# A final norm's weight multiplied in at PSUM, and two block products made to run together

## The chip, the core and the metric

One core of a Trainium2 chip runs the whole kernel in one launch. The engines are TensorE (PE; its weight loads are PEld), VectorE (DVE), ScalarE (ACT), GpSimd (POOL) and SyncE (SP, which here only issues DMAs). The metric is the device time of one execution in microseconds, as the median of three runs.

## The reference

One layer of a backbone is applied to 128 context tokens and 512 latent tokens (640 in all, width 2048), with fp32 weights, and a last RMSNorm follows:

```python
def _layer(x, mod, s0, shift_fn, lp):
    sh1, sc1, g1, sh2, sc2, g2 = jnp.split(mod, 6, axis=-1)
    h = _rmsnorm(x, lp['norm1_g']) * (1.0 + sc1) + sh1
    p = h @ lp['w_in']
    o_a, s_fin = _rwkv7_bidir(shift_fn(p[..., :C_SHIFT], lp['mu_shift']), s0, lp)
    o_b = _chunk_gmlp(jax.nn.gelu(p[..., C_SHIFT:]), lp)
    x = x + g1 * (jnp.concatenate([o_a, o_b], axis=-1) @ lp['w_out'])
    h = _rmsnorm(x, lp['norm2_g']) * (1.0 + sc2) + sh2
    ff = (jax.nn.silu(h @ lp['w_ffn_gate']) * (h @ lp['w_ffn_up'])) @ lp['w_ffn_down']
    return x + g2 * ff, s_fin
...
    y_prompt = _rmsnorm(x_ctx, final_norm_g)
    y_sample = _rmsnorm(x_lat, final_norm_g)
```

`_rmsnorm(x, g)` is `x * rsqrt(mean(x*x) + 1e-6) * g`: a scale for each token, and a weight for each of the 2048 columns. `_rwkv7_bidir` holds a scan over tokens in both directions in which each step changes a 64 by 64 state for each of 16 heads; `_chunk_gmlp` mixes tokens in chunks of 128.

## The kernel before

Large products are made with split operands: a fp32 weight tile is cast to a shorter format on ACT (`hi`), DVE subtracts to get the rest (`lo = raw - hi`), and three products hi·hi, hi·lo, lo·hi are summed in PSUM. TensorE thus waits for a pair of `hi` (ACT) and `lo` (DVE) for each weight tile.

**The first stage (to about 1160 us of the span)** runs the input projection: `win` makes "wide" products of 320 tokens (`big`), in blocks of weight columns. Between them, generators ("mixers") issue the small work of the scan. `between(k)` is called after each group of three wide products, and gives each mixer a budget. A generator yields the estimated cost of what it issued. A yield of -1.0 ends its turn, and the next one comes only at a call with `many` set, which is every twelfth wide product. A framework with a scheduler of its own then puts the instructions of each engine in an order, so neighbours in the code need not be neighbours on the engine.

The scan is worked out in chunks of 64 tokens. For each chunk a 64 by 64 triangular matrix is inverted: `solve` inverts blocks of 16 on DVE, and `merge` joins them to 32 and then to 64. `merge` runs for 8 pairs of heads and both directions, 16 times. For each, `blk(lhs, rhs)` makes 32 by 32 products for ten chunks into a PSUM tile of the pool `pt_`, which has two buffers and also serves the transposes of other generators and the spatial products. The steps are: `M1` from `blk(A1, Tn)`, copied by ACT; `blk(TT, M1)` added into `Tn` by DVE (L832); `blk(M1, TT)` added into `TF` by DVE (L837, L838); then the two products to 64 (`pM2`, L845, and `pT2`, L854), with ACT copies.

**The feed-forward part** uses one level of Strassen's method: `seven` makes seven products instead of eight, in the order `PORD = (1, 2, 3, 7, 5, 6, 4)`, and a hook for each product takes it out of PSUM, three or four products later (`lag`). POOL subtracts weight tiles for the combined ones (L1516). The down projection runs in six chunks of its inner dimension. The accumulators of the 8 output steps `n` (256 columns each) lie in `acc`, seven slots of 320 columns for each `n`.

**In the last chunk** (n from 7 to 0, about 3160 to 3285 us) `filled` first brings the accumulated slots back into PSUM (ACT, L1900), and the hook is `Last`. It puts the four quadrants together in two tiles `cd` (L1852, L1857, L1860 to L1863, L1868), adds the residual `x1d`, which SP loads for each step (`out`, L1841), and in hook 6 loads 256 columns of the last norm's weight, repeated over the partitions, into a free slot of `acc` (L1866). One step later `rows` transposes the two tiles to token rows in PSUM (`prd`, L1881), copies them to `acc` on ACT (L1882), and squares them on ACT with a sum for each token (L1885).

**The end** adds the sums of squares (L1946), takes the inverse root on POOL (L134), and scales. Each of ten half rows (128 tokens by 1024 columns) is multiplied by its token's scale and by the weight: six by one DVE instruction (L1958), four by ACT (L1955) and then POOL (L1956). SP stores each (L1959).

Of the kernel before, what the change touches and what calls it, by code (L numbers as in the profile page):

```python
# [86 lines left out]
def flow_step(ctx: ExitStack, tc, x_prompt, x_sample, state_rwkv, c, c_ctx, w_mod, b_mod,  # L87
# [706 lines left out]
    def merge(p, d2):  # L794

        GB = pairs[p].GB
        for gq in range(8):
            b = 16 * (gq % 2)
            BQ.dma_start(TB[16 * gq:16 * gq + 16, :, :, :, b:b + 16].rearrange("p d c w b -> p (d c w) b"),
                         d2[gq].rearrange("d c w a b -> a (d c w) b"))  # L800
        for h in range(2):
            base = 64 * (1 - h)
            for d in range(2):
                S.copy(A1_[base:base + 16, d, :, 16:32], GB[d][base:base + 16, :, 16:32])
                S.copy(A1_[base + 32:base + 48, d, :, 16:32], GB[d][base + 32:base + 48, :, 48:64])
        yield HOLD
        for d in range(2):
            GBd = GB[d]
            TF = bp.tile([P, NCH, CH], F32, tag="TF", name="TF")
            for h in range(2):  # L810
                G.memset(TF[hi32(h), :, 0:32], 0.0)
            Tn, TT, A1 = TB[:, d, :, 0, :], TB[:, d, :, 1, :], A1_[:, d]

            def blk(lhs, rhs, rows=range(4)):
                ps = pt_.tile([P, NCH, 32], F32, tag="pt", name="pblk")
                for cc in range(NCH):
                    for a_ in rows:
                        s = slice(32 * a_, 32 * a_ + 32)
                        TE.matmul(ps[s, cc, :], lhs[s, cc, :], rhs[s, cc, :], start=True, stop=True,  # L819
                                  tile_position=(32 * a_, 32 * a_))  # L820
                return ps

            M1 = bp.tile([P, NCH, 32], F32, tag="M1", name="M1")
            yield -1.0
            ps = blk(A1, Tn)
            S.copy(M1, ps)
            yield 1.6
            yield -1.0

            ps = blk(TT, M1, (0, 2))  # L830
            for h in range(2):
                V.tensor_add(Tn[lo32(h)], ps[lo32(h)], Tn[lo32(h)])  # L832
            yield 1.6
            yield -1.0
            ps = blk(M1, TT)
            for h in range(2):
                V.tensor_add(TF[lo32(h), :, 0:32], ps[lo32(h)], TT[lo32(h)])  # L837
                V.tensor_add(TF[hi32(h), :, 32:64], ps[hi32(h)], TT[hi32(h)])  # L838
            yield 1.7
            M2 = bp.tile([P, NCH, 32], F32, tag="M1", name="M2")  # L840
            yield -1.0
            ps = pt_.tile([P, NCH, 32], F32, tag="pt", name="pM2")
            for cc in range(NCH):
                for h in range(2):
                    TE.matmul(ps[hi32(h), cc, :], GBd[lo32(h), cc, 32:64], Tn[lo32(h), cc, :],  # L845
                              start=True, stop=True, tile_position=(64 * (1 - h), 64 * (1 - h) + 32))
            for h in range(2):
                S.copy(M2[hi32(h), :, :], ps[hi32(h), :, :])
            yield 1.2
            yield -1.0  # L850
            ps = pt_.tile([P, NCH, 32], F32, tag="pt", name="pT2")
            for cc in range(NCH):
                for h in range(2):
                    TE.matmul(ps[lo32(h), cc, :], M2[hi32(h), cc, :], TF[hi32(h), cc, 32:64],  # L854
                              start=True, stop=True, tile_position=(64 * (1 - h) + 32, 64 * (1 - h)))
            for h in range(2):
                S.copy(TF[lo32(h), :, 32:64], ps[lo32(h), :, :])
            yield 1.2
            BQ.dma_start(d_S[p, :, d, :, F_T:F_T + CH], TF)
            merged.append(p)  # L860
        G.memset(TB[:, :, :, 0, 0:16], 0.0)
# [936 lines left out]
    acc = dn.tile([P, 8, 7 * HALF], F32, name="acc")  # L1798
    sse = dn.tile([P, NT, 8], F32, name="sse")
    slot = lambda n, i: acc[:, n, (i - 1) * HALF:i * HALF]  # L1800

    def seg(h):

# [28 lines left out]
    class Last:  # L1832
# [11 lines left out]
        def __call__(self, o, p):  # L1844
            n, ps = self.n, self.ps
            ps[PORD[o]] = p
            if o == 1:
                self.xs = xqs.pop(n)
                self.cs = [xap.tile([P, T], F32, tag=next(ctags), name="cd") for _ in range(2)]
                self.tp = tp = xap.tile([P, 2, HALF], F32, tag="rs2", name="tp")  # L1850
                S.copy(tp[:, 0], ps[1])
                V.tensor_add(self.cs[0][:, t1], ps[2], tp[:, 0])  # L1852
                self.out(0, 0)
            elif o == 4:
                act = self.cs[1]
                S.copy(act[:, t2], ps[5])
                V.tensor_add(act[:, t1], ps[3], act[:, t2])  # L1857
            elif o == 5:
                act, pa, pq = self.cs[1], self.tp[:, 0], self.tp[:, 1]
                V.tensor_add(pq, ps[6], pa)  # L1860
                V.tensor_add(act[:, t1], act[:, t1], pq)
                V.tensor_add(pq, ps[7], pq)
                V.tensor_add(act[:, t2], act[:, t2], pq)  # L1863
                self.out(1, 0)
            elif o == 6:
                nc.sync.dma_start(acc[:, n, 5 * HALF:5 * HALF + 256],  # L1866
                                  final_norm_g[n * 256:(n + 1) * 256].partition_broadcast(P))
                V.tensor_add(self.cs[0][:, t2], ps[4], self.tp[:, 1])  # L1868
                later.append((2, lambda: (self.out(1, 1), self.out(0, 1))))
                later.append((ROWO, self.rows))  # L1870
                load_x1(n - 1)

        def rows(self):

            n, cs = self.n, self.cs
            for q0 in (0, 2, 4):
                nt = min(2, NT - q0)
                pr = pP.tile([P, 2, 256], F32, tag="P", name="prd")
                for t in range(nt):
                    for m in range(2):  # L1880
                        TE.transpose(pr[:, t, m * P:(m + 1) * P], cs[m][:, (q0 + t) * P:(q0 + t + 1) * P], ident)  # L1881
                S.copy(acc[:, n, q0 * 256:(q0 + nt) * 256].rearrange("p (t c) -> p t c", c=256), pr[:, 0:nt])  # L1882
                for t in range(nt):
                    junk = dn.tile([P, 256], F32, tag="junk", name="junk2")
                    S.activation(junk, pr[:, t], AF.Square, accum_out=sse[:, q0 + t, n:n + 1])  # L1885
# [60 lines left out]
    V.tensor_reduce(out=rs, in_=sse, axis=AX.X, op=ALU.add)  # L1946
    V.tensor_scalar(rs, rs, 1.0 / D, RMS_EPS, op0=ALU.mult, op1=ALU.add)
    rsqrt(rs, rs)
    fg = acc[:, :, 5 * HALF:5 * HALF + 256]
    for t in range(NT):  # L1950
        for h in range(2):
            out = fin.tile([P, 4, 256], F32, tag=f"out{h}", name="out")
            src, f = (ap[:, 4 * h:4 * h + 4] for ap in (acc[:, :, t * 256:(t + 1) * 256], fg))
            if t == 1 or t == 3:
                S.activation(out, src, AF.Copy, scale=rs[:, t:t + 1])  # L1955
                G.tensor_tensor(out=out, in0=out, in1=f, op=ALU.mult)  # L1956
            else:
                V.scalar_tensor_tensor(out=out, in0=src, scalar=rs[:, t:t + 1], in1=f, op0=ALU.mult, op1=ALU.mult)  # L1958
            nc.sync.dma_start(yrows(t)[:, h * 1024:h * 1024 + 1024], out.rearrange("p n c -> p (n c)"))  # L1959
    xax.close()  # L1960

# [28 lines left out]
```

## Time and profile before

| what | us |
|---|---|
| median of 3 runs | 3313.23 (3312.97 to 3317.33) |
| the profiled execution | 3309.26, its span 3307.5 |
| TensorE busy | 3147.1 |
| DVE busy | 2441.1 |
| ACT busy | 1457.4 |
| POOL busy | 1264.7 |
| mean granted TensorE clock | 0.981 of full speed |

Rows of the profile read as follows. In a timeline: start, duration, engine, source line, operation, output<-inputs, shape, count, and in brackets the idle time before it with what ended it. In a listing by line or tile: shortest/median/longest duration in ns, then the first and last start. In a table of waits: the sum, the number and the longest. Names leave out buffer numbers (`P` is a PSUM bank of the feed-forward part, `pM` is `pM2`, `t` is `t3`). In the rows of an order (not a time) `[waits ...]` names the engines or queues whose semaphores an instruction waits for.

### The profile page before, as it was taken

What the parts mean: (1) busy time and instruction counts of PE and PEld (TensorE: products, weight loads), DVE (VectorE), ACT (ScalarE), POOL (GpSimd) and SP (SyncE); (2) the same over time, 40 slices, a digit from 0 to 9 for tenths busy, and PEclk for the clock granted to TensorE, in tenths of its full rate; (3) what the DMA queues carried; (4) which work ended last, traced back from release to release, by engine and by line L of the source; (5) the groups of instructions that cost most, each with busy time, mean ns of one, the idle gap of its engine ahead of it and who ended that gap; (6) DMA issues with size and microseconds to landing.
All of it is one profiled execution on the core that took longest, in us unless ns stands there. A gap on an engine that the chain in (4) does not pass through costs nothing.

```text
span 3307.5 us, 72626 instructions
## 1 busy us (share of the span) xinstructions
PE 3147.1 (95%) x28216; PEld 2907.3 (88%) x28216; DVE 2441.1 (74%) x4356; ACT 1457.4 (44%) x3190; POOL 1264.7 (38%) x1114
## 2 busy tenths in 40 slices
PE   6899999999999999999899999999999999999996
PEld 3688787788877888888899999999999999999996
DVE  4548667876876678768887887777877788877787
ACT  3334444444443444334644444444444444444365
POOL 0001122212222113333156566566566555555543
PEclk8899999999999999999999999999999999999998
DMA  8767676677677588735543443433433454553453
GB/s 319 240 183 217 172 209 187 163 206 200 184 190 210 142 272 277 239 119 159 160 123 102 131 124 105 131 120 109 128 119 114 126 183 147 159 163 119 133 159 118
DMA packets 739376, 550.90 MB, mean 167 GB/s; under 512 B 140968, under 2 KB 673464, under 8 KB 730200
## 3 DMA queue, kind: packets, MB, share of 16 engines
q1 hardware_dynamic: 726712, 532.57, 53.8%
q0 software_dynamic: 9984, 13.13, 1.8%
q8 instruction: 222, 3.64, 0.5%
q14 instruction: 122, 1.00, 0.1%
q10 hardware_dynamic: 2336, 0.57, 0.1%
HBM read 437.79 MB, written 110.95 MB: 166 GB/s over the span
## 4 chain that ended last, share of the span: by engine, by line
PE 74%; DVE 11%; issue 6%; DMA 4%; POOL 3%; ACT 2%; DVEq 0%; SPq 0%; ACTq 0%; POOLq 0%
PE P L1605 15%; PE P L1604 15%; PE P L1603 15%; PE big L187 5%; PE big L189 4%; PE big L188 4%; PE pG L635 2%; PE pm L880 2%; DMA wt<-in_w_mod_dram 1%; DVE lo L1393 1%; PE big L1012 1%; PE pblk L819 1%; PE pXT L652 1%; DVE mx L780 1%; DMA raw<-in_w_out_dram 1%
## 5 line engine op out<-in xcount | busy, mean ns | idle before, releaser
L1603 PE MATMUL P<-xo,hi 128*128 128x320 f32 x2352 | 727.6, 309 | 3.3 <-ACT hi L1392 3.3
L1605 PE MATMUL P<-xo,lo 128*128 128x320 f32 x2352 | 727.6, 309 | 2.0 <-DVE lo L1393 1.9
L1604 PE MATMUL P<-xo,hi 128*128 128x320 f32 x2352 | 727.4, 309 | 0.0
L1393 DVE TENSOR_TENSOR lo<-raw,hi 128x512 fp32r<-128x512 f32 x532 | 511.7, 965 | 171.3 <-ACT hi L1392 165.9
L1392 ACT CAST hi<-raw 128x512 fp32r<-128x512 f32 x532 | 330.8, 622 | 495.9 <-PE P L1604 395.9
L187 PE MATMUL big<-h_hi,hi 128*128 128x320 f32 x1376 | 451.7, 328 | 6.6 <-ACT h_hi L343 3.7
L1603 PEld LDWEIGHTS P<-xo,hi 128*128 128x128 f32 x2352 | 442.1, 188 | 3.5 <-ACT hi L1392 3.5
L1605 PEld LDWEIGHTS P<-xo,lo 128*128 128x128 f32 x2352 | 441.9, 188 | 2.8 <-DVE lo L1393 2.8
L1604 PEld LDWEIGHTS P<-xo,hi 128*128 128x128 f32 x2352 | 442.1, 188 | 0.0
L189 PE MATMUL big<-h_hi,lo 128*128 128x320 f32 x1376 | 435.7, 317 | 2.6 <-DVE lo L166 2.5
L188 PE MATMUL big<-h_lo,hi 128*128 128x320 f32 x1376 | 435.4, 316 | 0.5 <-DVE h_lo L344 0.5
L1516 POOL TENSOR_TENSOR raw<-raw 128x512 f32<-128x512 f32 x252 | 407.5, 1626 | 14.3 <-DVE lo L1393 2.7
L1605 PE MATMUL P<-xd,lo 128*128 128x320 f32 x1232 | 384.0, 312 | 14.9 <-DVE lo L1393 14.6
L1603 PE MATMUL P<-xd,hi 128*128 128x320 f32 x1232 | 382.6, 311 | 4.4 <-ACT P L1900 1.9
L1604 PE MATMUL P<-xd,hi 128*128 128x320 f32 x1232 | 381.2, 309 | 0.0
L166 DVE TENSOR_TENSOR lo<-raw,hi 128x512 fp32r<-128x512 f32 x268 | 185.3, 694 | 214.1 <-ACT hi L165 202.8
L187 PEld LDWEIGHTS big<-h_hi,hi 128*128 128x128 f32 x1376 | 263.7, 192 | 72.9 <-issue 47.7
L1392 ACT CAST hi<-rawd 128x512 fp32r<-128x512 f32 (+1 forms) x288 | 169.0, 588 | 243.5 <-PE P L1604 204.9
L165 ACT CAST hi<-raw 128x512 fp32r<-128x512 f32 x268 | 165.5, 619 | 245.5 <-PE big L188 116.3
L189 PEld LDWEIGHTS big<-h_hi,lo 128*128 128x128 f32 x1376 | 263.5, 192 | 8.1 <-DVE lo L166 4.3
L188 PEld LDWEIGHTS big<-h_lo,hi 128*128 128x128 f32 x1376 | 264.2, 192 | 6.9 <-issue 3.5
L1605 PEld LDWEIGHTS P<-xd,lo 128*128 128x128 f32 x1232 | 231.8, 188 | 21.2 <-DVE lo L1393 21.1
(378 smaller groups left out, 6300.9 us busy)
## 6 DMA issues: line engine op xcount, KB each, us to landing
wt<-in_w_mod_dram SPq DMA_DIRECT2D x96, 1024.0 KB
raw<-in_w_ffn_gate_dram SPq DMA_DIRECT2D x182, 256.0 KB
raw<-in_w_ffn_up_dram SPq DMA_DIRECT2D x182, 256.0 KB
rec<-d_S SPq DMA_DIRECT2D x80, 576.0 KB
raw<-in_w_in_dram SPq DMA_DIRECT2D x172, 256.0 KB
rawd<-in_w_ffn_down_dram SPq DMA_DIRECT2D x128, 256.0 KB
raw<-in_w_out_dram SPq DMA_DIRECT2D x96, 256.0 KB
xd<-d_os SPq DMA_DIRECT2D x66, 320.0 KB
```

The source lines that it names most:

```text
L165: S.copy(hi, raw)
L166: V.tensor_sub(lo, raw, hi.bitcast(F32))
L187: TE.matmul(halves[hf], hi[:, k, :], h_hi[:, kb, s], start=(kb == 0), stop=False)
L188: TE.matmul(halves[hf], hi[:, k, :], h_lo[:, kb, s], start=False, stop=False)
L189: TE.matmul(halves[hf], lo[:, k, :], h_hi[:, kb, s], start=False, stop=(kb == KB - 1))
L635: TE.matmul(two[h][:, cc - c0, :], XZ[:, cc, h, :, :].rearrange("p s t -> p (s t)"), R[:, cc, :, :].rearrange("p s t -> p (s t)"), start=T ...
L1392: S.copy(hi[:, 0:nk], raw[:, 0:nk])
L1393: V.tensor_sub(lo[:, 0:nk], raw[:, 0:nk], hi[:, 0:nk].bitcast(F32))
L1516: G.tensor_tensor(out=o[:, 0:nk], in0=p[:, 0:nk], in1=q[:, 0:nk], op=ALU.subtract)
L1603: TE.matmul(ps, hi[:, k, :], xk[:, 0, :], start=f, stop=False)
L1604: TE.matmul(ps, hi[:, k, :], xk[:, 1, :], start=False, stop=False)
L1605: TE.matmul(ps, lo[:, k, :], xk[:, 0, :], start=False, stop=l)
```

## The change

- In `merge`, `blk(TT, M1)` and `blk(M1, TT)` are issued together, and DVE's additions of both follow. The yields between them go.
- In `Last`, the weight's load moves from hook 6 to hook 4.
- In `rows`, ACT's copy out of PSUM becomes a DVE multiply by the weight, with the same output.
- At the end each half row is only scaled by token: the second halves by ACT, the first by DVE. POOL takes no part.

```diff
-            ps = blk(TT, M1, (0, 2))
+            ps, ps2 = blk(TT, M1, (0, 2)), blk(M1, TT)
             for h in range(2):
                 V.tensor_add(Tn[lo32(h)], ps[lo32(h)], Tn[lo32(h)])
-            yield 1.6
-            yield -1.0
-            ps = blk(M1, TT)
+            ps = ps2
             for h in range(2):
                 V.tensor_add(TF[lo32(h), :, 0:32], ps[lo32(h)], TT[lo32(h)])
                 V.tensor_add(TF[hi32(h), :, 32:64], ps[hi32(h)], TT[hi32(h)])
-            yield 1.7
+            yield 3.3
...
+    fg = lambda n: acc[:, n, 5 * HALF:5 * HALF + 256]
...
             elif o == 4:
+                nc.sync.dma_start(fg(n), final_norm_g[n * 256:(n + 1) * 256].partition_broadcast(P))
                 act = self.cs[1]
...
             elif o == 6:
-                nc.sync.dma_start(acc[:, n, 5 * HALF:5 * HALF + 256],
-                                  final_norm_g[n * 256:(n + 1) * 256].partition_broadcast(P))
                 V.tensor_add(self.cs[0][:, t2], ps[4], self.tp[:, 1])
...
-                S.copy(acc[:, n, q0 * 256:(q0 + nt) * 256].rearrange("p (t c) -> p t c", c=256), pr[:, 0:nt])
+                V.tensor_tensor(out=acc[:, n, q0 * 256:(q0 + nt) * 256].rearrange("p (t c) -> p t c", c=256),
+                                in0=pr[:, 0:nt], in1=fg(n).unsqueeze(1).to_broadcast([P, nt, 256]), op=ALU.mult)
                 for t in range(nt):
                     junk = dn.tile([P, 256], F32, tag="junk", name="junk2")
                     S.activation(junk, pr[:, t], AF.Square, accum_out=sse[:, q0 + t, n:n + 1])
...
-    fg = acc[:, :, 5 * HALF:5 * HALF + 256]
     for t in range(NT):
         for h in range(2):
             out = fin.tile([P, 4, 256], F32, tag=f"out{h}", name="out")
-            src, f = (ap[:, 4 * h:4 * h + 4] for ap in (acc[:, :, t * 256:(t + 1) * 256], fg))
-            if t == 1 or t == 3:
+            src = acc[:, 4 * h:4 * h + 4, t * 256:(t + 1) * 256]
+            if h:
                 S.activation(out, src, AF.Copy, scale=rs[:, t:t + 1])
-                G.tensor_tensor(out=out, in0=out, in1=f, op=ALU.mult)
             else:
-                V.scalar_tensor_tensor(out=out, in0=src, scalar=rs[:, t:t + 1], in1=f, op0=ALU.mult, op1=ALU.mult)
+                V.tensor_scalar_mul(out, src, rs[:, t:t + 1])
```

The lines move by up to three: L1841 is L1840 in the changed kernel, L1393 is L1391, L1885 is L1884, and L1880 is the new multiply.

## The prediction

> **What bounds the kernel now.** I read the page first: TensorE is busy for 95% of the span and holds 74% of the chain that ended last, VectorE (DVE) 11%. So a change matters where TensorE waits for something, and after its last product.
>
> ```profile
> PE 3147.1 (95%) x28216; PEld 2907.3 (88%) x28216; DVE 2441.1 (74%) x4356; ACT 1457.4 (44%) x3190; POOL 1264.7 (38%) x1114
> ...
> PE 74%; DVE 11%; issue 6%; DMA 4%; POOL 3%; ACT 2%; DVEq 0%; SPq 0%; ACTq 0%; POOLq 0%
> ```
>
> The change touches three places, so I then took busy times by stretch: the stage with the merges (300 to 1160 us), a full output step of the last chunk (16.08 us) and its last one, and the end.
>
> ```profile
> 300.00:1160.00 860.00, 817.49 (x9808) 697.52 (x9807) 615.32 (x1227) 380.60 (x831) 184.22 (x285) 0.98 0.69 187
> 3231.96:3248.04 16.08, 15.23 (x103) 14.44 (x102) 13.77 (x23) 10.39 (x32) 5.31 (x4) 1.00 0.27 81
> 3264.10:3280.00 15.90, 15.57 (x107) 15.02 (x106) 12.38 (x24) 11.17 (x35) 2.66 (x2) 1.00 0.17 51
> ...
> 3289.00:3290.00 1.00, 0.00 (x0) 0.00 (x0) 1.00 (x1) 1.00 (x2) 1.00 (x1) 0.50 0.46 184
> 3296.00:3297.00 1.00, 0.00 (x0) 0.00 (x0) 1.00 (x1) 0.00 (x0) 1.00 (x1) 0.50 1.01 401
> 3305.00:3306.00 1.00, 0.00 (x0) 0.00 (x0) 0.00 (x0) 0.00 (x0) 0.00 (x0) 0.50 0.95 377
> ```
>
> After the clock of the first column come PE, PEld, DVE, ACT, POOL, granted clock, DMA share, GB/s. TensorE is idle for 42.5 us of the merge stage, 5%. In the last chunk DVE is nearly as full as TensorE. In the end only DVE, POOL and the stores work, and the stores are at 401 GB/s when they run.
>
> **The end.** The timeline of the end, by engine:
>
> ```profile
> 3281.78 1.26 DVE L1841 SCALAR_TENSOR_TENSOR cd<-cd,modc,x1d 128x64 f32<-128x64 f32 x4
> 3282.06 0.39 ACT L1885 ACTIVATE junk<-prd 128x256 f32<-128x256 f32 x1
> 3282.57 0.39 ACT L1885 ACTIVATE junk<-prd 128x256 f32<-128x256 f32 x1
> 3283.57 0.58 ACT L1882 COPY acc<-prd 128x512 f32<-128x512 f32 x1 [0.52 <-PE prd L1881]
> 3285.71 0.20 DVE L1946 TENSOR_REDUCE rse<-sse 128x5 f32<-128x40 f32 x1 [2.67 <-ACT junk L1885]
> 3287.40 15.69 DVE L1958 SCALAR_TENSOR_TENSOR out<-acc,rse 128x1024 f32<-128x1024 f32 x6 [1.29 <-POOL rse L134]
> 3288.62 12.19 POOL L1956 TENSOR_TENSOR out<-out,acc 128x1024 f32<-128x1024 f32 x4 [1.26 <-ACT out L1955]
> 3288.75 14.70 SPq L1959 DMA_DIRECT2D out_dram<-out  x10
> ...
> L1958 DVE SCALAR_TENSOR_TENSOR out<-acc,rse x6: 1272/3356/3455, 3287.4 to 3301.8; 128x1024 f32<-128x1024 f32 x6
> ...
> L1955 ACT ACTIVATE out<-acc,rse x4: 1132/1132/1149, 3287.4 to 3290.5; 128x1024 f32<-128x1024 f32 x4
> ...
> L241 DVE TENSOR_SCALAR xall<-xall,rs x5: 1286/1286/1289, 11.0 to 26.9; 128x2048 f32<-128x2048 f32 x5
> ```
>
> One DVE product of this size took 1.27 us alone and 3.36 us beside POOL, so ten outputs were spread over 15.7 us and the ten stores followed them. The change takes the second operand and POOL away. L241 is the new DVE form at twice the width, 1.29 us, so one is 0.65 us; five on DVE take 3.3 us, five on ACT 5 x 1.13 = 5.7 us, side by side. Then the stores bound: 10 x 0.524 MB at 401 to 406 GB/s are 12.9 to 13.1 us. From the first scale to the end that is 0.65 + 0.07 to the issue + 0.8 until bytes flow (issued at 3288.75, and only 0.46 of the DMA engines' time in the stretch from 3289) + 12.9 + 1.6 after the last byte = 16.0 us, where it was 3307.5 - 3287.4 = 20.1: 4.1 us less.
>
> Ahead of it something is lost. The order of ACT for the last output step shows it; L1884 is the square that was L1885:
>
> ```order
> L1899 COPY P_40345<-acc 128x320 [waits DVE_49,PE_49]
> L1884 ACTIVATE junk_40325,sse<-prd 128x256 [waits DVE_49]
> L1884 ACTIVATE junk_40327,sse<-prd 128x256 [waits Activation_49]
> L1884 ACTIVATE junk_40335,sse<-prd 128x256 [waits DVE_49,Activation_49]
> L1884 ACTIVATE junk_40337,sse<-prd 128x256 [waits Activation_49]
> L1884 ACTIVATE junk_40343,sse<-prd 128x256 [waits DVE_49,Activation_49]
> L1884 ACTIVATE junk_40396,sse<-prd 128x256 [waits DVE_49,Activation_49]
> ```
>
> In before, ACT copied the rows and squared them, waiting for nobody between; now the first square of each PSUM tile waits for DVE's multiply out of the same tile, and what is queued behind it on ACT (the next chunk's `hi` casts, the bank fills) waits too. In the last step DVE reaches that multiply when its four L1841 end, at 3283.04. The first multiply takes 0.60 us (below) and five squares at 0.51 (3282.06 to 3282.57) follow it: 3283.7 + 2.6 = 3286.3, where the reduction began at 3285.71: 0.6 us later. The end gives 4.1 - 0.6 = **-3.5**. Bounds: -4.6 if the squares were not held and only lost the copy ahead of them (0.5 us of the 0.58 of L1882); -2.6 with the stores 0.3 us and the squares 0.6 us slower.
> [...]
>
> **The last chunk.** One step of DVE, POOL and SP before:
>
> ```profile
> 3233.43 1.23 DVE L1841 SCALAR_TENSOR_TENSOR cd<-cd,modc,x1d 128x256 f32<-128x256 f32 x1
> 3234.57 1.58 DVE L1863 TENSOR_TENSOR cd<-cd,tp 128x320 f32<-128x320 f32 x1
> 3237.28 0.68 DVE L1393 TENSOR_TENSOR lo<-rawd,hi 128x512 fp32r<-128x512 f32 x1
> 3237.88 1.74 DVE L1841 SCALAR_TENSOR_TENSOR cd<-cd,modc,x1d 128x64 f32<-128x64 f32 x2
> 3239.54 1.78 DVE L1393 TENSOR_TENSOR lo<-t,hi 128x512 fp32r<-128x512 f32 x1
> 3241.24 0.67 DVE L1841 SCALAR_TENSOR_TENSOR cd<-cd,modc,x1d 128x64 f32<-128x64 f32 x2
> 3241.83 0.48 DVE L1852 TENSOR_TENSOR cd<-P,tp 128x320 f32<-128x320 f32 x1
> 3244.99 0.68 DVE L1841 SCALAR_TENSOR_TENSOR cd<-cd,modc,x1d 128x256 f32<-128x256 f32 x2 [1.48 <-DMA x1d<-d_x]
> 3248.04 0.49 DVE L1860 TENSOR_TENSOR tp<-P,tp 128x320 f32<-128x320 f32 x1 [0.76 <-PE P L1605]
> ...
> 3233.07 1.30 POOL L1516 TENSOR_TENSOR t<-rawd 128x512 f32<-128x512 f32 x1 [8.39 <-DMA rawd<-in_w_ffn_down_dram]
> 3234.45 1.36 POOL L1516 TENSOR_TENSOR rawd<-rawd 128x512 f32<-128x512 f32 x1
> 3238.04 2.73 POOL L1516 TENSOR_TENSOR rawd<-rawd 128x512 f32<-128x512 f32 x2 [2.23 <-DVE lo L1393]
> ...
> L750 DVE TENSOR_TENSOR sp<-psp,bsp x16: 269/485/699, 301.7 to 1166.0; 128x512 f32<-128x512 f32 x8, 128x128 f32<-128x128 f32 x8
> ...
> L1866 SPq DMA_DIRECT2D acc<-in_final_norm_g_dram x8: 332/454/772, 3161.1 to 3274.9; - x8
> ```
>
> DVE was busy 13.77 of 16.08 us, waited 1.48 us for `x1d` and 0.76 us for TensorE. About 4 us of the busy time is four operations stretched while POOL ran (1.23, 1.58, 1.74, 1.78 instead of 0.4, 0.4, 0.6, 0.6 by their unstretched neighbours). The new multiply is nearest to L750, PSUM times a repeated SBUF operand: 0.70 us for 512 columns, 0.60 from start to start as L1393; per step 0.60 + 0.60 + 0.35 = 1.55 us. Where it stands in DVE's order, one step from the `lo` pair behind the `x1d` wait on, before:
>
> ```order
> L1393 TENSOR_TENSOR lo<-rawd,hi 128x512 x2
> L1857 TENSOR_TENSOR cd<-P_39826,cd 128x320
> L1860 TENSOR_TENSOR tp<-P_39903,tp 128x320
> L1861 TENSOR_TENSOR cd<-cd,tp 128x320
> L1862 TENSOR_TENSOR tp<-P_39851,tp 128x320
> L1841 TENSOR_SCALAR cd<-cd,modc_90,x1d 128x256
> L1863 TENSOR_TENSOR cd<-cd,tp 128x320
> L1841 TENSOR_SCALAR cd<-cd,modc_90,x1d 128x64
> L1393 TENSOR_TENSOR lo<-rawd,hi 128x512
> L1868 TENSOR_TENSOR cd<-P_39957,tp 128x320
> ```
>
> and now:
>
> ```order
> L1391 TENSOR_TENSOR lo<-rawd,hi 128x512 x2
> L1880 TENSOR_TENSOR acc<-prd,acc 128x512 x2
> L1880 TENSOR_TENSOR acc<-prd,acc 128x256
> L1857 TENSOR_TENSOR cd<-P_39827,cd 128x320
> L1860 TENSOR_TENSOR tp<-P_39903,tp 128x320
> L1391 TENSOR_TENSOR lo<-rawd,hi 128x512
> L1861 TENSOR_TENSOR cd<-cd,tp 128x320
> L1862 TENSOR_TENSOR tp<-P_39852,tp 128x320
> L1840 TENSOR_SCALAR cd<-cd,modc_90,x1d 128x256
> L1391 TENSOR_TENSOR lo<-rawd,hi 128x512
> L1863 TENSOR_TENSOR cd<-cd,tp 128x320
> ```
>
> The multiplies come just ahead of L1860, where DVE had 0.76 us to spare, and the next `lo` moved forward, so TensorE, which waits for it, loses nothing. 1.55 - 0.76 leaves 0.8 us. From that I take 0.4: the stretched operations are four as before, but more of POOL's 5.3 us now falls on operations that read PSUM or on the `x1d` wait. The `x1d` wait stays: L1841 frees the tile about as long ahead. Six of the seven steps that hold a multiply are so full (the last has 12.38 us of DVE work in 15.90), 6 x 0.4 = **+2.4**. Bounds: all 1.55 us on the path, +9.3; TensorE's waits shrink by the earlier `lo` and a step loses 0.6 us, -3.6. The load of the weight moves from hook 6 to hook 4 but stands between the same two loads in SP's order, its last issue at 3274.9 some 8 us ahead of the reader at 3283; POOL's order of the chunk's subtractions stays. I cost both at nothing; if the load were late, it would hold DVE and, behind it, ACT's squares.
>
> **The merges.** TensorE's order at the last merge, before (`pblk` is a block product, its operand `M` the tile `M1`; `big` a wide product):
>
> ```order
> L189 MATMUL big<-h_hi,lo 128x320
> L819 MATMUL pblk<-M_13339,TB 32x32 x20
> L187 MATMUL big<-h_hi,hi 128x320
> L188 MATMUL big<-h_lo,hi 128x320
> L189 MATMUL big<-h_hi,lo 128x320
> L187 MATMUL big<-h_hi,hi 128x320
> ```
>
> Eight more wide ones follow there before the second block. And now:
>
> ```order
> L189 MATMUL big<-h_hi,lo 128x320
> L819 MATMUL pblk<-M_13339,TB 32x32 x20
> L819 MATMUL pblk<-TB,M_13339 32x32 x40
> L187 MATMUL big<-h_hi,hi 128x320
> L188 MATMUL big<-h_lo,hi 128x320
> ```
>
> What a change from wide to small and back costs is in the timeline; waits of TensorE there below it:
>
> ```profile
> 1136.97 0.31 PE L188 MATMUL big<-h_lo,hi 128*128 128x320 f32 x1
> 1137.12 0.31 PE L189 MATMUL big<-h_hi,lo 128*128 128x320 f32 x1
> 1137.35 0.82 PE L819 MATMUL pblk<-M,TB 32*32 32x32 f32 x40
> 1138.10 0.41 PE L187 MATMUL big<-h_hi,hi 128*128 128x320 f32 x1
> 1138.36 0.31 PE L188 MATMUL big<-h_lo,hi 128*128 128x320 f32 x1
> ...
> PE pM L845 <- DVE TF L838: 4.5, 1, 4.5
> ...
> PE pblk L819 <- DVE TB L832: 1.2, 2, 1.1
> ```
>
> Wide ones start every 0.15 us; here 0.23 passes before the block and 0.26 after it: 0.19 us for one break. Thirteen of 16 pairs stood apart, but some second blocks stood beside other small products, where the break stays; I take ten, 1.9 us. The two waits of the second block for L832 (1.2 us) go, since it no longer follows that addition. Against this, both PSUM buffers of the pool are now held until six DVE additions are done, and twice a spatial product follows within nine wide ones: +0.6. Sum **-2.5**; bounds -7.6 (no +0.6, and the 4.5 us wait of `pM2` goes too) and +3 (two waits of 1.5 us for a buffer, nothing gained).
>
> **Sum.** -3.5 + 2.4 - 2.5 = -3.6 us. The profiled execution took 3309.26 us (span 3307.5), so 3305.7; its time is 4.0 us under the median of the runs, 3313.23, and from that median I forecast **3309.6**. A measurement of this kernel can tell about 0.2% from no change, 6.6 us, so the forecast is no change.
>
> **Rivals.**
> - Faster. The steps take their lower bound (-3.6), the merges -5, the end -3.5: -12.1, 3301. For it: TensorE's chain through DVE in a step gets shorter. Against: DVE has 1.55 us more in a full step. 0.30.
> - Slower. DVE becomes the bound of the last chunk. If POOL's operations meet two more of DVE's operations per step, each 1.1 us longer (1.58 for L1863 instead of 0.48), a step costs 0.4 + 2.2 = 2.6, six 15.6; with -6.0 elsewhere +9.6, 3323. It decides from 2.1 us a step. For it: DVE's 13.77 us plus 1.55 and the `x1d` wait are 16.8. Against: the multiply reads PSUM, as L1852 and L1860, which kept 0.48 and 0.49. 0.18.
> - The end doesn't shorten, since the stores can't keep 400 GB/s: 3.5 us less gain, 3313. It lies within the forecast's band.
>
> **How the numbers follow.** The forecast, within 0.2%, has 0.52, the rivals 0.30 and 0.18. The range is 3300 to 3322: it takes in the faster rival and the slower one up to 1 us short of its price. Left out are the ends that need all bounds on one side: -4.6 - 3.6 - 7.6 = -15.8, 3297, and -2.6 + 9.3 + 3 = +9.7, 3323; I give them 0.05 and 0.10.
>
> **What would show it.** Right: the first scale at about +0.6 us against the last product, ten outputs within 6 us, stores without a gap; steps of 16.2 to 16.9 us; the two block products back to back. Wrong: steps under 16 us or over 18; a last store more than 17 us after the first scale; a merge stage that moves by more than 6 us.

## The result

The changed kernel took 3326.11 us (median of 6 runs, 3317.51 to 3331.07) beside 3313.1 us of the kernel before (6 runs, 3301.86 to 3317.33): a ratio of 1.0038, 95% interval 1.0022 to 1.0054. That is slower by 12.6 us (7 to 18); 3309.6 had been forecast, with a range up to 3322. The profiled execution took 3326.0 us, its span is 3324.0.

The page of the changed kernel:

```profile
PE 3151.0 (95%) x28216; PEld 2914.3 (88%) x28216; DVE 2442.9 (73%) x4379; ACT 1453.1 (44%) x3167; POOL 1252.4 (38%) x1110
q8 instruction: 222, 3.64, 0.5%
```

The engines work as long as before (TensorE +3.9 us, DVE +1.8), and the span is 16.5 us longer: the time is in waits. To place it I took five marks from the timelines: TensorE's 1500th product of 320 or more columns (at about 320 us), the last wide product of the input projection, the start of the last chunk, TensorE's last wide product, the end. Between them (us):

| kernel | to 1500th | merges | middle | last chunk | after it |
|---|---|---|---|---|---|
| before | 320.3 | 829.5 | 2010.6 | 120.6 | 26.6 |
| after | 319.6 | 841.2 | 2012.0 | 127.3 | 24.0 |
| difference | -0.8 | +11.7 | +1.4 | +6.7 | -2.6 |

**The end** is as forecast, less a part. The timeline of the end of the changed kernel:

```profile
3302.91 1.74 DVE L1880 TENSOR_TENSOR acc<-prd,acc 128x512 f32<-128x512 f32 x3
3303.68 0.38 ACT L1884 ACTIVATE junk<-prd 128x256 f32<-128x256 f32 x1 [3.11 <-DVE acc L1880]
3306.21 0.20 DVE L1945 TENSOR_REDUCE rse<-sse 128x5 f32<-128x40 f32 x1 [1.56 <-ACT junk L1884]
3307.90 5.31 ACT L1953 ACTIVATE out<-acc,rse 128x1024 f32<-128x1024 f32 x5 [1.72 <-POOL rse L134]
3307.90 3.40 DVE L1955 TENSOR_SCALAR out<-acc,rse 128x1024 f32<-128x1024 f32 x5 [1.29 <-POOL rse L134]
```

Ten outputs take 5.3 us instead of 15.7 (one on DVE took 0.75 us, where 0.65 had been forecast), and from the first scale to the end it is 16.1 us (forecast 16.0, before 20.1). But ACT waits 3.11 us for the first multiply, and from the last product (3300.03) to the reduction it is 6.2 us, where it was 4.8.

**The last chunk.** What DVE waits for there, in the changed kernel and then in before:

```profile
DVE cd L1840 <- DMA x1d<-d_x: 14.6, 8, 3.1
DVE lo L1391 <- ACT hi L1390: 4.4, 9, 1.1
DVE tp L1860 <- PE P L1603: 0.2, 1, 0.2
```

```profile
DVE cd L1841 <- DMA x1d<-d_x: 11.7, 8, 2.2
DVE tp L1860 <- PE P L1605: 5.1, 5, 1.9
DVE lo L1393 <- ACT hi L1392: 3.1, 3, 1.1
```

and the busy times of the chunk, changed kernel first (columns as in the prediction):

```profile
3172.73:3300.03 127.30, 115.45 (x772) 111.76 (x771) 108.40 (x186) 67.08 (x183) 41.49 (x29) 0.99 0.36 108
```

```profile
3160.32:3280.91 120.59, 114.49 (x773) 110.23 (x771) 100.67 (x167) 74.44 (x206) 40.76 (x29) 1.00 0.39 113
```

DVE has 7.7 us more to do. Its wait for TensorE (5.1) is used up, and its wait for `x1d` didn't shrink but grew by 2.9. DVE busy and waiting for `x1d` are 123.0 of 127.3 us: DVE and the load that it releases are the bound. That the load (L1829) is released by DVE shows in SyncE's waits in this stretch:

```profile
SPq L1829 <- DVE cd L1840: 73.9, 14, 12.0
```

TensorE now waits for ACT, which fills banks late (its squares wait 13.3 us for DVE's multiply, in the chunk and behind it). TensorE's waits in the last chunk and behind it, those of over 0.3 us in sum:

```profile
PE P L1601 <- ACT P L1899: 11.8, 12, 1.5
PE prd L1879 <- DVE cd L1840: 1.7, 2, 1.2
PE P L1898 <- ACT junk L1884: 0.5, 1, 0.5
```

**The merges.** TensorE's waits from 300 to 1172 us in the changed kernel (the rows that grew or are new), and in before:

```profile
PE pG L635 <- DVE XZ L618: 14.2, 12, 2.4
PE pm L878 <- DMA wt<-in_w_mod_dram: 6.5, 4, 2.1
PE psp L749 <- DVE TB L832: 4.6, 2, 3.2
PE pblk L819 <- issue: 3.7, 5, 1.2
PE big L187 <- ACT hi L165: 2.9, 2, 1.6
```

```profile
PE pG L635 <- DVE XZ L618: 10.3, 8, 2.4
PE pm L880 <- DMA wt<-in_w_mod_dram: 3.5, 2, 2.9
```

The 4.5 us wait of `pM2` and the block's wait for L832 are gone, as hoped. New are 4.6 us in which a spatial product (`psp`) waits for a PSUM buffer that L832 has to free, and 3.7 us that name nobody (`issue`), inside the pair itself. Over the stage TensorE's waits add up to 50.2 us instead of 42.2. And a wait can cost more than its length. The timeline of TensorE around the first `psp` wait, and the granted clock (the column behind the busy times) ahead of it, in it and behind it:

```profile
520.81 0.30 PE L189 MATMUL big<-h_hi,lo 128*128 128x320 f32 x1
524.27 1.51 PE L749 MATMUL psp<-wspT,vt 128*128 128x128 f32 x8 [3.16 <-DVE TB L832]
525.43 0.61 PE L187 MATMUL big<-h_hi,hi 128*128 128x320 f32 x1
525.84 0.47 PE L188 MATMUL big<-h_lo,hi 128*128 128x320 f32 x1
526.11 0.47 PE L189 MATMUL big<-h_hi,lo 128*128 128x320 f32 x1
```

```profile
519.78:521.12 1.34, 1.33 (x9) 1.07 (x8) 1.34 (x4) 0.00 (x0) 0.00 (x0) 1.00 0.84 289
524.90:528.30 3.40, 3.40 (x16) 3.40 (x15) 3.24 (x6) 1.00 (x2) 0.06 (x1) 0.50 0.00 0
528.30:530.00 1.70, 1.70 (x8) 0.68 (x7) 0.99 (x2) 0.80 (x2) 1.12 (x2) 1.00 0.20 41
```

For 3.4 us after the wait the clock is at 0.50, and wide products start every 0.27 us instead of 0.15. Summed over the stage from the trace's clock records, TensorE had half its clock for 54.6 us, where it was 41.0. At (0.267 - 0.147) / 0.267 = 45% lost, 13.6 us more are 6.1 us, by estimate. With 8.0 us of longer waits that is 14.1, against 11.7 seen; the prediction's 1.9 us of saved breaks would fit in between, but no run measures them alone.
In the changed kernel's clock records the half clock comes in stretches of 3.4, 6.8, 10.2 and 13.6 us, and of 22.9 us at the end. A wait of 1.86 us (ending at 1100.57 us) was followed by half clock from 1101.7 to 1105.1. It is no rule by length: behind waits of 1.81 and 2.29 us (ending at 979.98 and 2801.97 us) the clock stayed full.

### The profile page after: what moved, and what is told of

Same layout as the page of the kernel before. It is cut to its first block, busy times and chain, and to the rows that moved or that the text cites. A ratio compares the mean times of both kernels' runs of the same rounds, so it can differ in the third digit from the quotient of the medians.

```text
span 3324.0 us, 72630 instructions
## 1 busy us (share of the span) xinstructions
PE 3151.0 (95%) x28216; PEld 2914.3 (88%) x28216; DVE 2442.9 (73%) x4379; ACT 1453.1 (44%) x3167; POOL 1252.4 (38%) x1110
## 3 DMA queue, kind: packets, MB, share of 16 engines
q8 instruction: 222, 3.64, 0.5%
## 4 chain that ended last, share of the span: by engine, by line
PE 60%; DVE 8%; issue 5%; DMA 3%; POOL 2%; ACT 1%; SPq 0%; POOLq 0%; ACTq 0%; DVEq 0%
PE P L1603 15%; PE P L1601 14%; PE P L1602 14%; PE big L187 2%; PE big L189 2%; PE big L188 2%; DVE lo L1391 1%; PE pG L635 1%; PE big L1010 1%; PE big L1448 1%; PE big L1446 1%; PE big L1447 1%; PE pm L878 1%; DMA d_S<-GR 1%; PE big L1011 1%
## 5 line engine op out<-in xcount | busy, mean ns | idle before, releaser
L1391 DVE TENSOR_TENSOR lo<-raw,hi 128x512 fp32r<-128x512 f32 x532 | 521.4, 983 | 161.8 <-ACT hi L1390 156.8
L1601 PE MATMUL P<-xd,hi 128*128 128x320 f32 x1232 | 384.0, 312 | 14.1 <-ACT P L1899 11.8
L166 DVE TENSOR_TENSOR lo<-raw,hi 128x512 fp32r<-128x512 f32 x268 | 186.0, 696 | 214.4 <-ACT hi L165 205.9
L1601 PEld LDWEIGHTS P<-xd,hi 128*128 128x128 f32 x1232 | 233.1, 189 | 17.4 <-ACT P L1899 14.9
```

What stands on the lines that cost most here:

```text
L166: V.tensor_sub(lo, raw, hi.bitcast(F32))
L1391: V.tensor_sub(lo[:, 0:nk], raw[:, 0:nk], hi[:, 0:nk].bitcast(F32))
L1601: TE.matmul(ps, hi[:, k, :], xk[:, 0, :], start=f, stop=False)
```

## The experiments

Theories at the start: in the merges, "slots" (both PSUM buffers held), "place" (the merges are a turn shorter, so everything behind them meets elsewhere) and, from the third run on, "instruction fetch"; in the last chunk, "ACT is held" and "DVE is full". Each ratio is against before on the same chip. Beside it stand its interval and what the trace says: "first part" is from the same 1500th product to the first feed-forward product. In seven kernels with the merges untouched it was 1326.6 to 1335.1 us, mean 1331; the merge stage in them 829.5 to 832.3; in fourteen with the norm's rows untouched the last chunk was 120.6 to 122.0 us.

### The two halves of the change

> Only the merge edit (pair issued together, yields between removed), norm as before. If the merge stage lost the 12 us that the trace of the changed kernel shows there (the wide products of the feed-forward part start 12.6 us later): 3325 us, +12 against before. If those 12 us were an accident of one profiled execution and the norm edits cost it all: 3311 to 3313.

Edit: before with the first hunk of the change alone. Measured: 3322.51 us, ratio 1.0014 (1.0002 to 1.0025); merge stage 839.1 us, first part 1338.5, half clock in the stage for 54.6 us. So the merge edit loses by itself, and loses in the merge stage; less than the +12 that was expected.

> Only the norm edits (multiply in PSUM rows, earlier load, scaled end), merges as before. By the traces: last chunk +6.7 us, end -2.6, sum +4: 3317 us, seven steps of 16.6 to 17.5 us with TensorE waiting for ACT's bank fills. If the last chunk's loss came from what the merge had shifted: 3309.6, steps of 16.1 to 16.5 us.

Edit: the other hunks alone. Measured: 3320.87 us, ratio 1.0007 (0.9991 to 1.0023), not settled by the time; the trace has merges of 829.8, last chunk 126.3, end 24.0 us. The last chunk's loss has nothing to do with the merges. In the profiled executions the halves are about -2.6 at the end, +5 to 6 in the last chunk (against a usual 121.4) and +7 to 11 in the first part: 10 to 14 us, which agrees with the 12.6 measured.

### Merges: slots, place, or instructions

> Merge edit with the pace of before: pair and all additions together, but the yields 1.6, -1.0 and 1.7 kept behind them, so that what follows the pair stands where it stood. Theory 'slots' (both PSUM buffers of the pool held by the pair make a spatial product wait, and the clock drops after it): still +8 to +12, 3321 to 3325. Theory 'place' (the merge is a turn shorter, so its later steps and the other generators meet elsewhere): -3 to +3, 3310 to 3316.

```diff
-            yield 3.3
+            yield 1.6
+            yield -1.0
+            yield 1.7
```

(on the merge edit alone). Measured: 3335.61 us, ratio 1.0051 (1.0032 to 1.0069); first part 1353.2 us, +22. Neither theory said that. "Place" in the form that the old pace would restore the time has fallen. What grew most is the wait without a releaser; two rows of TensorE's waits in this kernel:

```profile
PE pblk L819 <- issue: 9.1, 6, 3.3
PE psp L749 <- DVE TB L832: 1.5, 1, 1.5
```

The slot wait is smaller than in the changed kernel and the loss twice as large. In the trace's DMA records each such wait of over 0.4 us inside a pair ends 1.2 to 1.5 us after a 16 KB packet of the instruction queue has ended, here and in the changed kernel. That made the third theory: a pair is 60 products, each of which the trace shows as two weight loads and two products, 240 instructions in some 1.5 us where nothing holds them (with the old pace 112 of a pair's 120 product instructions ran from 716.88 to 718.32 us, ahead of the 3.3 us wait), more than TensorE may have fetched ahead; that it fetches ahead was a guess.

> Before with the blocks a turn apart as before, but the first block's DVE additions moved behind the second block, so that both PSUM buffers are held together and longer than in the changed kernel, with no run of 60 small products. Theory 'slots': spatial products and other transposes wait for a buffer, 4 us or more, stage 836 to 845 us, total +6 to +15. Theory 'instruction fetch' (the run of 60 small products uses up TensorE's loaded instructions; its waits without a releaser inside the pair are 3.7 us in the changed kernel and 9.3 with the old pace, each ending 1.2 to 1.5 us after a 16 KB packet of the instruction queue): waits without releaser below 0.6 us, stage within 4 us of 829.5.

```diff
-            ps = blk(TT, M1, (0, 2))
-            for h in range(2):
-                V.tensor_add(Tn[lo32(h)], ps[lo32(h)], Tn[lo32(h)])
+            ps1 = blk(TT, M1, (0, 2))
             yield 1.6
             yield -1.0
             ps = blk(M1, TT)
+            for h in range(2):
+                V.tensor_add(Tn[lo32(h)], ps1[lo32(h)], Tn[lo32(h)])
```

Measured: 3316.48 us, ratio 1.0009 (0.9998 to 1.002), merge stage 832.6 us, waits without releaser in the blocks 1.2 us (under 0.6 had been expected), 0.4 us of `psp` for DVE, and 1.1 us in which a block waits for a buffer that L750 frees. Holding both buffers longer than the change does costs 3 us at most in the stage; the first part, 1336.9 us, is just outside the usual. "Slots" in this form is not the main cause, though the 4.6 us in the changed kernel are real: whether they come depends on what stands behind the pair. A pair also has to find two free buffers at once, and this run does not test that.

> Control for 'place': before with the merges only due earlier (14 instead of 18 as their due time), blocks apart as before. If the merge stage of 829.5 us (last wide product minus start of the mixing stage, the same within 0.4 us in three kernels with the merges as before) is a lucky place and any displacement costs some 10 us: 835 to 842 us, total +5 to +12. If the pairing itself costs it: 826 to 833 us, total within 4 us.

> Second control for 'place': before with the estimated cost of a merge at 22 instead of 18, which gives the merges a larger budget and moves them forward, blocks apart as before. 'Place is worth 10 us': the start of the feed-forward products moves by 5 us or more, total 3318 to 3326. 'Pairing costs it': within 4 us of before.

```diff
-        mixM.add(merge(p, d2), 18.0)
+        mixM.add(merge(p, d2), 14.0)
```

(and 22.0). The number is the estimated cost of a merge, from which its budget comes, not a due time as the first of these expectations says; with 14 the merges fall later, behind the last wide product. Measured: 0.9986 (0.9971 to 1.0001) and 0.9993 (0.9978 to 1.0009), first parts 1329.6 and 1329.8 us. With 14 the merge stage itself, 815.6 us, is no fair mark, since its last wide product came sooner. Moving the merges costs nothing in these two placements. That any displacement costs 10 us has fallen too; that some does is not excluded.

> The merge edit (pair issued together, yields removed) at another placement, with the merges' estimate at 14. If pairing costs something wherever it is put: +4 to +10 us against the kernel with that estimate and the blocks apart (0.9986), so 3314 to 3320 us. If its cost belongs to the one placement: within 3 us of it, 3308 to 3312 us.

Measured: 3330.82 us, 1.0047 (1.0029 to 1.0065), first part 1356.6 us, 27 more than with the same estimate and the blocks apart. The pair costs at a second placement, and more. (+4 to +10 had been expected.) Here `pm` waits 9.2 us for its weights, and two more rows of TensorE's waits are

```profile
PE pblk L819 <- DVE sp L750: 6.1, 4, 2.5
PE pblk L819 <- issue: 3.3, 5, 1.1
```

against this one with the same estimate and the merge edit left out:

```profile
PE pblk L819 <- issue: 5.9, 3, 3.9
```

There the order put a block of 20 and one of 40 products back to back at 639 us, and inside that row TensorE waited 3.9 us. So waits without a releaser can come where blocks stand together, with the edit or without, but the loss in the first part does not follow their size: 5.9 us of them went with no loss, 3.3 with 27 us, 4.6 (the merge edit alone) with 7, 9.1 (old pace) with 22. The pair at this estimate waits for buffers too, and TensorE has half its clock for 68.3 us of the stage, against 30.7 with the blocks apart.

### Does a row of small products outrun its instructions?

> A measurement: the kernel with the end on DVE alone, and behind TensorE's last transpose 512 products of 32 by 32 in a row into a free PSUM tile, which nobody reads. Theory 'instruction fetch': 512 products need more instructions than are loaded ahead, so the row breaks into pieces with idle time without releaser between them, each piece starting 1.2 to 1.5 us after a 16 KB packet of the instruction queue has landed; mean over 10 ns per instruction. Rival (the waits in the merges have another cause): the row runs through, at the 10 to 12 ns per instruction of the merges' blocks (120 in 0.8 us).

Not answered: the row ran through without a gap, but at 52 ns a product instruction, 26 ns an instruction with the weight loads, the clock being at 0.50 from 3290 us on. That is far slower than a block of the merges (80 instructions in 0.82 us in the prediction's timeline, 10 ns each). All products here used one tile of the array; the next run changes that.

> The measurement again with 512 products of 32 by 32 that go round the four diagonal tiles of the array, as the merges' do (the row on one tile took 26 ns per instruction and so never asked for a 256-instruction packet more often than each 6.7 us). 'Instruction fetch': at the merges' 8 ns per instruction the row runs ahead of the packets and breaks into pieces of some 256 instructions, with idle time of over 0.5 us without releaser between them. Rival: runs through.

```diff
+    for k in range(512):
+        s, c = slice(32 * (k % 4), 32 * (k % 4) + 32), 32 * (k // 4 % 10)
+        TE.matmul(burst[s, c:c + 32], ident[s, 0:32], ident[s, 0:32], start=True, stop=True,
+                  tile_position=(32 * (k % 4), 32 * (k % 4)))
```

TensorE's timeline of the row, and the instruction queue on this kernel's page:

```profile
3291.11 1.95 PE L1949 MATMUL burst<-ident 32*32 32x32 f32 x208
3295.32 1.28 PE L1949 MATMUL burst<-ident 32*32 32x32 f32 x128 [2.25 <-issue]
3298.79 1.93 PE L1949 MATMUL burst<-ident 32*32 32x32 f32 x128 [2.19 <-issue]
3303.90 1.93 PE L1949 MATMUL burst<-ident 32*32 32x32 f32 x128 [3.19 <-issue]
3309.02 1.93 PE L1949 MATMUL burst<-ident 32*32 32x32 f32 x128 [3.19 <-issue]
3312.76 1.93 PE L1949 MATMUL burst<-ident 32*32 32x32 f32 x128 [1.81 <-issue]
...
q8 instruction: 230, 3.77, 0.5%
```

Between the first and the last, these are pieces of exactly 128 product instructions (64 products of two passes; 256 instructions with their weight loads), with 1.8 to 3.2 us of idle time between them. The page has 230 instruction packets, before 222: eight more for the 2048 instructions that were added, so a packet is 256 instructions, and with 3.64 MB in 222 packets some 16 KB; the 56432 products and weight loads on the page of before are 220 times 256. In the DMA records these pieces start 1.3 to 1.5 us after a packet has ended. A new piece began every 5.1 us while the output's stores ran at some 400 GB/s (3299 to 3309 us), and every 3.7 us behind them. That TensorE's instructions come in such packets, and that 64 small products of two passes run quicker (1.3 to 1.9 us) than the next piece begins (3.5 to 5.1 us), is shown.

> The control for it: before, blocks apart, with the operands of the 32 by 32 products cut in the same way. Some 4 to 8 us faster than before by shorter blocks (three blocks a merge, 16 merges), 3305 to 3309 us.

> The merge edit alone, with the operands of the 32 by 32 products cut to their upper halves (bfloat16), so that each product is one weight load and one product instead of two of each: the same pairs, the same two PSUM buffers, half the instructions. 'Instruction fetch': waits without releaser inside the pair fall from 4.6 us to under 1 us. If these are what the pair costs, the pair costs within 3 us of the kernel with the blocks apart and the same operands; if slots and displaced steps cost it, 5 to 12 us more than that kernel remain.

```diff
+            def top(ap):
+                return ap.bitcast(mybir.dt.bfloat16)[:, 1::2]
...
-                        TE.matmul(ps[s, cc, :], lhs[s, cc, :], rhs[s, cc, :], start=True, stop=True,
+                        TE.matmul(ps[s, cc, :], top(lhs[s, cc, :]), top(rhs[s, cc, :]), start=True, stop=True,
```

Measured, blocks apart: 3293.32 us, 0.9942 (0.9921 to 0.9963), first part 1312.0. The pair: 3279.49 us, 0.9899 (0.988 to 0.9919), first part 1295.3. With half the instructions the pair is *faster* than the blocks apart, by 14 us, where it was slower by 5. Neither expectation for the pair (within 3 us, or 5 to 12 us slower) held, nor the one for the control: it is 19 us faster than before, not 4 to 8. TensorE is busy with the blocks for 23.5 us instead of 47.4.

Rows of TensorE's waits, the pair:

```profile
PE pblk L822 <- issue: 1.2, 1, 1.2
PE pm L881 <- DMA wt<-in_w_mod_dram: 1.1, 1, 1.1
```

the blocks apart with the same operands:

```profile
PE pblk L822 <- issue: 1.2, 1, 1.2
PE pm L883 <- DMA wt<-in_w_mod_dram: 7.6, 2, 4.4
```

and the merge edit with all instructions:

```profile
PE pblk L819 <- issue: 4.6, 5, 1.2
```

Against the pair with all instructions, the wait without a releaser fell by 3.4 us, TensorE's waits in the stage from 49.7 to 35.7 us, and its time at half clock from 54.6 to 30.7. Against the blocks apart with the same operands (43.6 and 44.4 us), the wait without a releaser is the same. The sum of waits fell by 7.9 us, and the row that fell most is `pm`'s wait for its weights, by 6.5; the edit doesn't touch `pm`, which only stands elsewhere in the order. The spatial products still wait for the merges' buffers (2.8 us in two rows). So pairing need not cost anything, and a pair of half the instructions hardly waits for them. But cutting the operands also halved the blocks' time, and the gain over the control lies in another wait. That the instruction fetch is the main price of the pair in full precision is argued, not shown; how much is luck of the order stays open.

### The last chunk: ACT held, or DVE full

> Norm edits alone, but rows leave PSUM by ACT's copy as in before, and DVE multiplies by the weight in place in SBUF; the squares on ACT follow the copy and wait for nobody. Theory 'ACT is held' (its squares wait for DVE's multiply, and its bank fills, for which TensorE waits 11.8 us in the last chunk, stand behind them): those waits fall to 2 to 4 us, steps to 16.0 to 16.5 us, last chunk 121 to 123 us, total -1 to -3 against before. Rival 'DVE is full': DVE has as much or more to do here (a multiply in SBUF can be stretched by POOL), steps stay at 17 us or more, last chunk 126 us or more, total +3.

```diff
-                V.tensor_tensor(out=acc[:, n, q0 * 256:(q0 + nt) * 256].rearrange("p (t c) -> p t c", c=256),
-                                in0=pr[:, 0:nt], in1=fg(n).unsqueeze(1).to_broadcast([P, nt, 256]), op=ALU.mult)
+                row = acc[:, n, q0 * 256:(q0 + nt) * 256].rearrange("p (t c) -> p t c", c=256)
+                S.copy(row, pr[:, 0:nt])
+                V.tensor_tensor(out=row, in0=row, in1=fg(n).unsqueeze(1).to_broadcast([P, nt, 256]), op=ALU.mult)
```

> Norm edits alone, with the squares ahead of DVE's multiply in the code, so that on the shared PSUM tile DVE waits for ACT and not ACT for DVE. 'ACT is held': ACT's fills come in time, waits for them 2 to 4 us, last chunk 121 to 123 us (a little more if DVE now waits for squares). 'DVE is full': 126 us or more as with the multiply first.

Edit of the second: the loop with the squares stands ahead of the multiply. Measured: 3311.97 us, 1.0002 (0.9987 to 1.0017), last chunk 125.0; and 3313.66 us, 0.9993 (0.9979 to 1.0007), last chunk 124.6. The times can't tell them from before, nor from the norm edits alone; the traces can. TensorE's waits in the last chunk with the norm edits alone, and then with the squares first:

```profile
PE P L1603 <- ACT P L1901: 12.7, 12, 1.4
```

```profile
PE P L1605 <- DVE lo L1393: 9.0, 10, 1.8
PE P L1603 <- ACT P L1901: 1.3, 1, 1.3
```

With ACT free its fills are in time, and TensorE waits for DVE's `lo` instead (6.5 us with the multiply in SBUF, where ACT's fills cost 1.6). Of the 5 us that the multiply costs (126.3 against 121.4), 1.3 to 1.7 go with ACT's wait; 3.1 to 3.6 stay as long as DVE has the work. Both theories hold a part, "DVE is full" the larger.

### What is faster than both

> Before with only the end changed: all ten half rows by one DVE instruction each with both operands, neither ACT nor POOL. Theory 'POOL stretches DVE': one takes 1.27 us instead of 3.36, the ten are done in 12.7 us beside stores of 12.9 us, end 3.4 us shorter, 3309.7 us. Rival 'the instruction is slow by itself in a row, or the stores bind already': 3312 to 3314.

```diff
-            if t == 1 or t == 3:
-                S.activation(out, src, AF.Copy, scale=rs[:, t:t + 1])
-                G.tensor_tensor(out=out, in0=out, in1=f, op=ALU.mult)
-            else:
-                V.scalar_tensor_tensor(out=out, in0=src, scalar=rs[:, t:t + 1], in1=f, op0=ALU.mult, op1=ALU.mult)
+            V.scalar_tensor_tensor(out=out, in0=src, scalar=rs[:, t:t + 1], in1=f, op0=ALU.mult, op1=ALU.mult)
```

Measured: 3307.32 us, 0.997 (0.9955 to 0.9986). The row of its ten outputs:

```profile
L1954 DVE SCALAR_TENSOR_TENSOR out<-acc,rse x10: 1279/1280/1285, 3293.5 to 3304.2; 128x1024 f32<-128x1024 f32 x10
```

1.28 us each, ten in 12.05 us beside stores that need as long (12.9 to 13.1 us at 401 to 406 GB/s). The end is 23.2 us instead of 26.6, 0.8 better than in the changed kernel, and the last chunk pays nothing. The 3.4 us are what theory "POOL stretches DVE" said; the ratio gives 5 to 15 us, and no trace here explains more than the 3.4.

> Candidate for a faster kernel: the end on DVE alone (measured at 0.997 of before) and the merges' estimate at 14 (0.9986). If the two add up: 0.9956, 3299 us. If the estimate's gain was scatter: 0.997, 3303 to 3304 us.

Measured: 3303.7 us, 0.9977 (0.9962 to 0.9991), an interval that holds the 3.4 us of the end: the estimate adds nothing that can be told.

> The two parts that gained, together: the pair issued together with the operands of the 32 by 32 products cut to their upper halves (0.9899 alone), and the end on DVE alone (0.997 alone). If they add up: 0.987, 3269 us; last product to the end 23.2 us instead of 26.6. If they share a gain: 0.989 to 0.990, 3276 to 3279 us.

Measured: 3275.97 us, 0.9885 (0.9865 to 0.9905), first part 1298.0, end 23.2 us: between the two expectations, and the interval holds both. It is the fastest run here, at the price of block products with bfloat16 operands. With all products in full precision it is the end on DVE alone.

## Why the prediction was wrong

- **The merges**: the term -2.5, bounds -7.6 to +3, was wrong in sign: +5 by the ratio for the merge edit alone (0.7 to 8.3, so the times alone don't exclude +3), and +9.6 and +11.7 in two profiled merge stages, out of the bounds. The sign of being wrong that the prediction had named, a merge stage that moves by more than 6 us, came. The step that failed is "What a change from wide to small and back costs is in the timeline", with 0.19 us saved per break: it took the breaks and two waits for all that the pair changes. TensorE's waits in the stage grew by 8.0 us instead. In them are 3.7 us without a releaser (put down to its instructions: each such wait of over 0.4 us ends 1.3 to 1.4 us after a packet), which had no term since 60 products were priced at the rate of a block of 20; 4.6 us for a PSUM buffer, where +0.6 was right in place (twice a spatial product waits) and mis-sized; and 3.9 and 3.0 us more for `pG` and `pm`, which the edit doesn't touch. And the clock had no term: 13.6 us more at half speed, some 6 us by the estimate above. The waits that were to go, `pM2` and L832, did go. That waits and clock make up the loss is shown; how much of it the instruction fetch causes stays open.
- **The last chunk**: the term +2.4 (0.4 a step). Six steps took 103.8 us instead of 95.6 between their L1860, +1.4 each (17.3 us, where 16.2 to 16.9 was named as the sign of being right), inside the bounds and close to the upper one, 1.55 "all on the path". The step "From that I take 0.4" failed: I let POOL's stretching and the `x1d` wait absorb half of what remained. The wait grew instead; the load is released by DVE itself. And the fills, which I had named as queued behind the squares, had no price.
- **The slower rival**: its headline, "DVE becomes the bound of the last chunk", holds, but by its own sign it did not come: it was to decide from 2.1 us a step, and a step cost 1.4. Its mechanism did not hold either: the multiplies are not stretched (0.69 us at most for 512 columns, 0.70 forecast), and POOL ran beside none of them. Its total of +9.6 had -6.0 elsewhere, where the runs show a loss, so that it lies near the measured +12.6 is luck.
- **The end**: -4.1 + 0.6 forecast, -4.0 + 1.4 measured, the lower bound of -2.6. The squares wait for DVE as the order had shown, but DVE reached the multiply 2.9 us after the last product, not 2.1. With the multiply in SBUF the squares don't wait for it; there the end is 22.6 us, 4.0 less than before, so the 1.4 us are the price of that wait.
- **ACT and DVE on one PSUM tile**: ACT's 3.11 us wait is the order of its squares behind DVE's multiply out of the same tile. With the squares first the wait changes sides (at the end DVE waits 1.00 us for ACT), and the last chunk is 1.7 us shorter. The runs show the wait and its price, not why the one waits for the other.

## What to carry to other kernels

Count the instructions of a run of small products, not only its time: a row that uses up several hundred in a few microseconds can wait for the next ones, as the measurement's did (256 in 1.3 to 1.9 us, then 1.8 to 3.2 us idle). Spread such products between large ones, or make each one pass. Price more waiting of TensorE at more than its length: here 8.0 us more came with 13.6 us more at half clock. And compare an edit with a control that has the same operands, wait by wait, before a change of sign is put down to one cause. Work that is taken off the end and put on an engine in the steady part pays only if that engine waits there for something that it doesn't itself release.

## What the runs showed of the hardware

- TensorE's instructions come in 16 KB packets of 256; in a long row of small products a piece began every 3.5 to 5.1 us, while its 256 instructions ran in 1.28 us (once) or 1.93 us (five times).
- In the changed kernel's merge stage waits of TensorE of 1.80 to 3.16 us (ending at 438.57 and 524.27 us) came with 3.4 or 6.8 us at a granted clock of 0.50, and two of 1.65 and 1.64 us, 3 us apart (ending at 449.25 and 452.33), with 13.6 us from the first one's end; in the last chunk one of 1.31 us (3217.94) with 3.4 us; others, of 1.81 and 2.29 us (979.98 and 2801.97), with none.
- One DVE product of two operands and a scalar over 1024 columns takes 1.28 us in a row of ten without POOL, and 3.36 in the median beside POOL (before): taking POOL's share away did more than sharing the work (ten outputs in 12.05 us, against 15.7).
